# Pairing the small-expert steps of a mixture-of-experts layer, and folding their partial sums behind the pair

## The chip, the core and the metric

The kernel runs on one core of a Trainium2 chip. The core has a matrix engine (PE, TensorE), three elementwise engines (DVE, ACT and POOL) and sixteen DMA engines, whose transfers are issued here by the SP queue and, for a few, by ACT. The engines run side by side and wait for each other through semaphores. The metric is the device time of one execution in microseconds (us).

## The reference

Two transformer layers over 256 latent tokens and 256 context tokens of width 1024. Each layer has a token mixer (neighbourhood attention, differential attention, short convolution) and a feed-forward part; layer 0 has a dense one, layer 1 a mixture of eight experts of which each token takes two. The change lies in that last part and in the final normalization:

```python
def swiglu(h, w1, w3, w2):
    return (jax.nn.silu(h @ w1) * (h @ w3)) @ w2          # 1024 -> 3584 -> 1024 in an expert

def moe_ffn(h, w_router, w1, w3, w2):
    logits = jnp.einsum('...d,de->...e', h, w_router)
    top_vals, top_idx = lax.top_k(logits, 2)
    top_w = jax.nn.softmax(top_vals, axis=-1)
    gates = jnp.sum(jax.nn.one_hot(top_idx, 8) * top_w[..., None], axis=-2)
    y = jnp.zeros_like(h)
    for e in range(8):
        y = y + gates[..., e:e + 1] * swiglu(h, w1[e], w3[e], w2[e])
    return y
...
x_lat = x_lat + g_f * moe_ffn(modulate(rms_norm(x_lat), sh_f, sc_f), ...)
return rms_norm(x_lat, final_gain)
```

All weights are fp32, so the experts' weights are by far the largest stream: 44 MB for one expert.

## The kernel before

The first half of the program (to about 870 us) is layer 0 and the mixer of layer 1; the change doesn't touch it. Then `route` sorts the experts by how many tokens chose them and gives each a rank. For the inputs used here the branch in `moe_main` (line 1846) is taken that treats ranks 0 and 1 as *heavy*, ranks 7, 2, 3, 4 and 5 as *light*, and leaves rank 6, which no token chose, out. Rank 7 is always expert 0, so that its weights can be fetched before the routing is known.

**Heavy experts** (`heavy`) are computed for all 256 tokens. Each 128x1024 piece of weights is cut into a rounded part `whi` (ACT, line 469) and the rest `wlo` (DVE, line 471), and each product is done as three fast ones (lines 222 to 224, tile `H`): `xh*whi`, `xl*whi`, `xh*wlo`. The pieces are cut one ahead of their use, in three buffers. One piece gives 24 products of 256 columns (first two weight matrices) or 12 of 512 columns (third matrix, where the operands are `gh`, `gl`). Groups of four 512-column blocks of PSUM are filled at a time (`by_bank`); the last two pieces of a group are used together, bank by bank, and so both must be cut before the second product set of that step.

**Light experts** (`light`) gather at most 32 or 64 tokens (`n` = 64 for rank 2, 32 for the others) and use the weights uncut, in plain fp32. With so few tokens the array is cut into column tiles: four tiles of 32 columns or two of 64, which work side by side on different rows of the weights, so that one PSUM bank (tile `L`) holds four (or two) partial sums. A plain fp32 product is two instructions in the profile. When a bank is done, ACT copies it to `s` (line 1649, `folded`), and later a *fold* sums the partial sums: products of `s` with a matrix of ones at the right places (tile `tg`), for `n` = 32 in four column tiles with a DVE transpose behind them (lines 1657 and 1661, tile `sT`, two buffers), for `n` = 64 as four full-width products with `s` as the loaded operand (line 1665). The result goes to `g`: by ACT with Silu for the first matrix (line 1668), by a DVE multiplication for the second (line 1670).

One light expert is 21 *steps* (the generator's `yield`s). A step (`quad`) uses four chunks of 512 KB. Steps 0 to 11 are pairs: steps 2k and 2k+1 fill the same two banks. Steps 12 and 13 fill one bank each. Steps 14 to 20 are the third matrix and fill two banks together. After step 20 the result is scattered to the tokens (`scatter`): it is scaled (`of`), cut into `oh` and `ol` (lines 469 and 471), and each token half gets two fast products with `selT` (lines 1528 and 1529), added to `xk` (tile `xT`) on DVE. The folds that wait are emitted after the first step of the next bank pair (`fold_all` at `u == 0`). `places` (transposes and small products that make `selT`, lines 1454 and 1456) and the gather of the next rank's tokens (line 1469) are small tasks put between steps by `some_tasks`.

**The order.** `mix_experts` weaves the two streams: a surplus of PE time over transfers decides whether a heavy step or light steps come next; light steps come in bursts of two (`BURST`), whatever bank they belong to. First eight steps of rank 7 run before the weave (`first_steps`). The products of both streams are chained in this written order; a scheduler then places every engine's instructions. Twenty 512 KB buffers (tile `raw`) form one ring for both streams: SP issues the next transfer when the oldest buffer is free.

**The end** (`finish_out`): squares of the result are summed on ACT, DVE multiplies all four quarters by the final gain, then 1/rms is worked out in small DVE steps, and two quarters are scaled by it on DVE and two on ACT, and stored.

Of the kernel before, what the change touches and what calls it, by code (L numbers as in the profile page):

```python
# [13 lines left out]
F32 = mybir.dt.float32  # L14
F32R = mybir.dt.float32r
# [8 lines left out]
KT = 8  # L24
# [15 lines left out]
PE_COST = {32: (1.05, 1.0), 64: (1.95, 1.9), 128: (3.75, 3.65)}  # L40
HEAVY = 2.85
WIN_W = 16
BURST = 2
GROUPS = (2, 2, 2, 1)


# [83 lines left out]
def tile_hybrid_block(ctx: ExitStack, tc: tile.TileContext, x, c, cx, c_ctx, ada_w, ada_b, w_in, w_out, na_rpb,  # L130
# [1239 lines left out]

    def first_steps():

        run = mo["run7"] = light((7,), 32)
        while len(mo["early"]) > TAIL:
            next(run)
            mo["run7_done"] = mo.get("run7_done", 0) + 1
        while mo["folds"]:
            mo["folds"].popleft()()
        mo["run7_tasks"] = list(tasks)
        tasks.clear()  # L1380
        mo["far"].close()
        mo["left"], mo["early"] = mo["early"], {}

    def pbank(tag):
        return mo["psum"].tile([128, 512], F32, name=tag, tag=tag, bufs={"H": 4, "L": 2, "tg": 2}[tag])
# [130 lines left out]
    def scatter(o, h, selT, gate, after):  # L1516

        big = mo["big"]
        of = gated(o, h, gate)
        oh = big.tile([128, 512], F32R, name="oh", tag="oh", bufs=2)  # L1520
        ol = big.tile([128, 512], F32R, name="ol", tag="ol", bufs=2)
        parts(of.rearrange("p a b -> p (a b)"), oh, ol)

        def add():
            for t in range(2):
                y = pbank("tg")
                s = selT[:, t * 128:(t + 1) * 128]
                pe.matmul(y, s, oh, start=True, stop=False)  # L1528
                pe.matmul(y, s, ol, start=False, stop=True)  # L1529
                accumulate(t, h, y.rearrange("p (a b) -> p a b", a=4))  # L1530
            if after is not None:
                after(h)
        mo["adds"].append(add)
        tasks.append(lambda: mo["adds"] and mo["adds"].popleft()())
# [88 lines left out]
    def light(ranks, n, last=None):  # L1623
# [16 lines left out]
        for i, r in enumerate(ranks):  # L1640
            v = {}

            def place(r=r, v=v):
                v["v"] = places(r, n)
            chunks = light_chunks(r)

            def folded(a, j, first):
                s = mo["pool"].tile([128, 512], F32, name="s", tag="s", bufs=2)
                act.activation(s, a, AF.Copy)  # L1649

                def fold():

                    gs = g[j]
                    p = pbank("tg")[:, :4 * n].rearrange("p (a b) -> p a b", a=4)
                    if n == 32:
                        for c in range(4):
                            chained(pe.matmul(p[32 * c:32 * c + 32], fold32,  # L1657
                                              s.rearrange("p (q c i) -> p c q i", c=4, i=32)[:, c], start=True,
                                              stop=True, tile_position=(0, 32 * c), skip_group_check=True))
                        t = mo["pool"].tile([128, 4, n], F32, name="sT", tag="sT", bufs=2)  # L1660
                        dve.transpose(out=t, in_=p)  # L1661
                        p = t
                    else:
                        for f in range(4):
                            chained(pe.matmul(p[:, f, :], s[:, f * 128:(f + 1) * 128], mo["fold", n], start=True,
                                              stop=True))
                    if first:
                        act.activation(gs, p, AF.Silu)
                    else:
                        dve.tensor_tensor(out=gs, in0=gs, in1=p, op=ALU.mult)  # L1670
                folds.append(fold)

            def fold_all():
                while folds:
                    folds.popleft()()

            def quad(banks, lhs, u, nk, per):

                raws = [weights(*next(chunks)) for _ in range(4)]
                for h, bank_ in enumerate(banks):  # L1680
                    for k in range(4 * per):
                        cs = (h if per == 1 else k % 2) * 512
                        product(bank_, lhs(4 * per * u + k), raws[k // per][:, cs:cs + 512], 4 * per * u + k, nk)

            def latents(kt, i=i):
                return x[:, kt, i * n:(i + 1) * n]

            def columns(f):
                return g[f // 4][:, f % 4, :]
            for j0, nj in col_groups(GROUPS):  # L1690
                for w in range(2):
                    a = [pbank("L") for _ in range(nj)]
                    for u in range(nj):
                        quad(a, latents, u, KT, 3 - nj)
                        if u == 0 and not (nj == 1 and w):
                            fold_all()
                        if u < nj - 1:
                            yield
                    for h in range(nj):
                        folded(a[h], j0 + h, w == 0)  # L1700
                    yield
                if j0 == 2:
                    tasks.append(place)
            end = i == len(ranks) - 1
            if end:
                mo["following"]()
            o = [pbank("L") for _ in range(2)]
            for u in range(7):
                quad(o, columns, u, 28, 1)
                if u == 0:  # L1710
                    fold_all()
                if u < 6:
                    yield
            if "v" not in v:
                tasks.remove(place)
                place()
            while mo["adds"]:
                mo["adds"].popleft()()
            for h in range(2):
                scatter(o[h], h, *v["v"], last if end else None)  # L1720
            yield

    def mix_experts(heavies, lights, end=True, begun=False):
# [3 lines left out]

        def pool(name, **kw):
            return s.enter_context(tc.tile_pool(name=name, side="right", **kw))
        mo["tight"] = any(n == 128 for _, n in lights)  # L1730
        if heavies:
            mo["split"] = pool("m_split", bufs=2 if mo["tight"] else 3)
# [39 lines left out]
        runs = {"light": light_groups()}  # L1772
        if heavies:
            runs["heavy"] = heavy(last, heavies)
        parts_of = {"heavy": deque([(HEAVY, 0.5)] * (84 * len(heavies))),
                    "light": deque((2 * PE_COST[n][k >= 14], 2.0) for r, n in lights for _ in r for k in range(21))}
        if begun:
            tasks.extend(mo["run7_tasks"])
            for _ in range(mo["run7_done"]):
# [4 lines left out]
        mean = sum(p[0] for p in both) / sum(p[1] for p in both)  # L1784

        total, surplus = len(both), START
        k, burst = "heavy", 0
        while runs:
            done = total - sum(len(q) for q in parts_of.values())
            lead = LEAD * max(done, 0) / total  # L1790

            if "heavy" not in runs or "light" not in runs:
                k = next(iter(runs))
            elif burst == 0:
                k = "heavy" if surplus <= lead else "light"
                burst = BURST if k == "light" else 1
            burst -= 1
            if next(runs[k], "end") == "end":
                del runs[k]
                continue  # L1800
            cost, load = parts_of[k].popleft()
            surplus += cost - mean * load
            if "heavy" not in runs:
                tasks.extend(gains)
                gains = []
            some_tasks(1 if len(tasks) < 4 else 2)
# [13 lines left out]

    def finish_out():
        squares(1)
        qs = {}
        for t in range(2):
            for h in range(2):
                hs = slice(4 * h, 4 * h + 4)
                q = qs[t, h] = mo["ring"][t][:, h, :].rearrange("p (k n) -> p k n", k=4)
                dve.tensor_tensor(out=q, in0=mo["xk"][t][:, hs, :], in1=mo["fg"][:, hs, :], op=ALU.mult)
        ms = sm(2)
        dve.tensor_tensor(out=ms, in0=mo["ss"][:, 0:2], in1=mo["ss"][:, 2:4], op=ALU.add)  # L1830
        dve.tensor_scalar(out=ms, in0=ms, scalar1=1.0 / D, scalar2=None, op0=ALU.mult)
        r = rsqrt(ms, 2)
        for t in range(2):
            for h in range(2):
                q = qs[t, h]
                if h:
                    act.activation(q, q, AF.Copy, scale=r[:, t:t + 1])
                else:
                    dve.tensor_scalar(out=q, in0=q, scalar1=r[:, t:t + 1], scalar2=None, op0=ALU.mult)
                (act if h else sy).dma_start(  # L1840
                    out=out[0, t * 128:(t + 1) * 128, h * 512:(h + 1) * 512].rearrange("p (k n) -> p k n", k=4), in_=q)

    def moe_main():
        route()
# [79 lines left out]
```

## Time and profile before

| | |
|---|---|
| time, median of 3 runs | 1692.32 us (1688.62 to 1694.82) |
| the profiled execution | 1694.52 us, of which the profile's span is 1692.7 us |
| PE busy | 1630.3 us, 96% of the span |
| DVE, ACT busy | 1026.3 us (61%), 639.4 us (38%) |
| bytes read from HBM | 431.66 MB, 256 GB/s over the span |
| granted PE clock, mean | 0.986 of full speed |

Times in rows count from the span's start. In a timeline row the second number is the length of the row's instructions together; products overlap, so that what a run of products costs PE is read from its start to the start of the next row. In `x16` the last number counts instructions.

### The profile page before, as it was taken

To read this page: it belongs to the slowest core of one execution; us is meant where nothing else is said; L and a number is where in the kernel's file an instruction comes from. 1 tells how busy PE (TensorE), PEld (TensorE's weight loads), DVE (VectorE), ACT (ScalarE), POOL (GpSimd) and SP (SyncE) were. 2 spreads that over 40 slices of the span, in tenths; PEclk is the share of its full clock that TensorE was granted. 3 is DMA by queue.
4 is the path that set the end of the run, shared out by engine and by line. 5 is a ranking of instruction groups with operands and counts; after the bars stand their busy time and mean duration, and the time that the engine had idled before them with its cause. 6 is when DMAs were issued, how large, how long until landed. Compare 5 with 4: busy or idle time off the path is not lost. (4 is left out here: it accounts for less than half of the span.)

```text
span 1692.7 us, 28524 instructions
## 1 busy us (share of the span) xinstructions
PE 1630.3 (96%) x10942; PEld 1268.0 (75%) x10942; DVE 1026.3 (61%) x2043; ACT 639.4 (38%) x1057; POOL 25.6 (2%) x43
## 2 busy tenths in 40 slices
PE   7999999999999999999989999999999999999996
PEld 4688777988778888988874866666878677878773
DVE  4768977888877784779963343214445545353454
ACT  4555544422212222465534322313333243333431
POOL 0100001000000000000010000000000000000000
PEclk9999999999999999999989999999999999999998
DMA  9743444266545553342499999989999989998994
GB/s 286 178 126 109 104 149 112 84 191 199 199 154 168 170 192 112 100 125 75 178 365 366 409 407 355 344 336 403 363 362 396 368 335 377 394 398 335 389 381 176
DMA packets 234193, 434.66 MB, mean 257 GB/s; under 512 B 23497, under 2 KB 142785, under 8 KB 234049
## 3 DMA queue, kind: packets, MB, share of 16 engines
q1 hardware_dynamic: 232560, 432.14, 71.5%
q8 instruction: 88, 1.44, 0.4%
q10 hardware_dynamic: 1488, 0.62, 0.1%
q14 instruction: 57, 0.46, 0.1%
HBM read 431.66 MB, written 1.05 MB: 256 GB/s over the span
## 5 line engine op out<-in xcount | busy, mean ns | idle before, releaser
L471 DVE TENSOR_TENSOR wlo<-raw,whi 128x1024 fp32r<-128x1024 f32 x168 | 202.9, 1223 | 235.7 <-ACT whi L469 218.9
L222 PE MATMUL H<-xh,whi 128*128 128x256 f32 x896 | 257.7, 288 | 2.6 <-ACT whi L469 1.8
L224 PE MATMUL H<-xh,wlo 128*128 128x256 f32 x896 | 254.9, 284 | 2.0 <-DVE wlo L471 1.9
L223 PE MATMUL H<-xl,whi 128*128 128x256 f32 x896 | 254.6, 284 | 0.0
L469 ACT ACTIVATE whi<-raw 128x1024 fp32r<-128x1024 f32 x168 | 174.3, 1054 | 181.9 <-PE H L223 92.4
L222 PE MATMUL mm<-hh,whi 128*128 128x512 f32 (+1 forms) x648 | 230.2, 356 | 1.7 <-ACT t2k L298 1.2
L223 PE MATMUL mm<-hl,whi 128*128 128x512 f32 (+1 forms) x648 | 226.4, 350 | 0.0
L224 PE MATMUL mm<-hh,wlo 128*128 128x512 f32 (+1 forms) x648 | 225.1, 348 | 0.0
L100 ACT ACTIVATE whi<-raw 128x1024 fp32r<-128x1024 f32 x130 | 134.6, 1056 | 238.6 <-DMA raw<-in_ffn_w_dram 139.4
L101 DVE TENSOR_TENSOR wlo<-raw,whi 128x1024 fp32r<-128x1024 f32 x130 | 157.1, 1220 | 56.5 <-ACT whi L100 55.6
L222 PEld LDWEIGHTS H<-xh,whi 128*128 128x128 f32 x896 | 172.5, 192 | 20.0 <-issue 9.3
L224 PEld LDWEIGHTS H<-xh,wlo 128*128 128x128 f32 x896 | 172.6, 193 | 3.0 <-DVE wlo L471 3.0
L223 PEld LDWEIGHTS H<-xl,whi 128*128 128x128 f32 x896 | 172.7, 193 | 0.2
L222 PEld LDWEIGHTS mm<-hh,whi 128*128 128x128 f32 x648 | 123.5, 191 | 21.3 <-ACT t2k L298 2.8
L1636 PE MATMUL L<-raw,xT 128*32 128x512 f32 (+1 forms) x896 | 137.2, 597 | 0.3
L224 PEld LDWEIGHTS mm<-hh,wlo 128*128 128x128 f32 x648 | 123.3, 191 | 15.1 <-issue 0.2
L223 PEld LDWEIGHTS mm<-hl,whi 128*128 128x128 f32 x648 | 123.8, 191 | 13.6
L322 DVE SCALAR_TENSOR_TENSOR ada_t<-raw,scol,ada_t 128x256 f32<-128x256 f32 x266 | 116.5, 480 | 2.8
L1649 ACT ACTIVATE s<-L 128x512 f32<-128x512 f32 x70 | 41.8, 597 | 151.0 <-PE L L1636 127.1
L222 PE MATMUL H<-whi,gh 128*128 128x512 f32 x224 | 90.2, 403 | 3.9 <-ACT gh L469 3.1
L1661 DVE STREAM_TRANSPOSE sT<-tg 128x128 f32<-128x128 f32 x56 | 15.5, 308 | 126.4 <-PE tg L1657 126.3
L223 PE MATMUL H<-wlo,gh 128*128 128x512 f32 x224 | 88.7, 396 | 0.9 <-DVE wlo L471 0.9
(320 smaller groups left out, 2764.2 us busy)
## 6 DMA issues: line engine op xcount, KB each, us to landing
raw<-in_moe_w_dram SPq DMA_DIRECT2D x572, 512.0 KB, 8.3
raw<-in_ada_w_dram SPq DMA_DIRECT2D x40, 1024.0 KB, 5.3
raw<-in_ffn_w_dram SPq DMA_DIRECT2D x32, 1024.0 KB, 5.4
raw<-in_w_in_dram SPq DMA_DIRECT2D x12, 1024.0 KB, 5.2
raw<-in_w_in_dram SPq DMA_DIRECT2D x24, 512.0 KB, 5.3
aw<-in_ada_w_dram SPq DMA_DIRECT2D x16, 512.0 KB, 7.3
far<-in_moe_w_dram SPq DMA_DIRECT2D x16, 512.0 KB, 7.3
raw<-in_w_out_dram SPq DMA_DIRECT2D x5, 1024.0 KB, 5.6
```

The lines of the kernel that those rows point to most:

```text
L100: self.nc.scalar.activation(hi, r, AF.Copy)
L101: self.nc.vector.tensor_tensor(out=lo, in0=r, in1=hi.bitcast(F32), op=ALU.subtract)
L222: return [pe.matmul(o, ah, bh, start=start, stop=False, **kw), pe.matmul(o, ah, bl, start=False, stop=False, **kw), pe.matmul(o, al, bh, s ...
L223: pe.matmul(o, ah, bl, start=False, stop=False, **kw),
L224: pe.matmul(o, al, bh, start=False, stop=stop, **kw)]
L322: dve.scalar_tensor_tensor(out=t[:, g, :], in0=raw[:, kt, :], scalar=scol[:, kt, g:g + 1], in1=t[:, g, :], op0=ALU.mult, op1=ALU.add)
L469: act.activation(hi, src, AF.Copy, scale=scale)
L471: dve.tensor_tensor(out=lo, in0=src, in1=hi.bitcast(F32), op=ALU.subtract)
L1636: chained(pe.matmul(o[c * n:(c + 1) * n, :], lhs, rhs, start=(k < ng), stop=(k >= nk - ng), tile_position=(0, c * n), skip_group_check=True))
L1649: act.activation(s, a, AF.Copy)
L1661: dve.transpose(out=t, in_=p)
```

## The change

Six edits, all behind the routing:

1. A light burst no longer counts two steps: it goes on until a step that ends a bank pair (odd steps, and step 20, which is a burst by itself).
2. Steps 12 and 13 fill two banks that are held together; their folds come after both.
3. Waiting folds are emitted after the *second* step of a pair (`u == 1`) and no longer after the first; only where light steps run without heavy ones (`mo["alone"]`: `first_steps`, and branches not taken here) it stays at the first.
4. The fold for `n` = 64 also goes in column tiles of 32, in two halves of the columns, with two DVE transposes; `sT` has one buffer instead of two.
5. The scatter of the very last light rank isn't cut in `oh` and `ol`: one plain fp32 product with `of` takes the place of two.
6. In `finish_out` only two quarters are multiplied by the gain early; the other two are scaled and multiplied in one DVE instruction at the end.

```diff
-BURST = 2
...
     def first_steps():
+        mo["alone"] = True
...
     def scatter(o, h, selT, gate, after):
-        parts(of.rearrange("p a b -> p (a b)"), oh, ol)
+        of = of.rearrange("p a b -> p (a b)")
+        if after is None:
...
+            parts(of, oh, ol)
...
+                if after is None:
+                    pe.matmul(y, s, oh, start=True, stop=False)
+                    pe.matmul(y, s, ol, start=False, stop=True)
+                else:
+                    pe.matmul(y, s.bitcast(F32), of, start=True, stop=True)
...
-                    if n == 32:
...
-                        t = mo["pool"].tile([128, 4, n], F32, name="sT", tag="sT", bufs=2)
-                        dve.transpose(out=t, in_=p)
+                    if n < 128:
+                        t = mo["pool"].tile([128, 4, n], F32, name="sT", tag="sT", padded_shape=[128, 4, 64])
+                        p = p.rearrange("p (a b) -> p a b", b=32)
+                        for h in range(n // 32):
+                            for c in range(4):
+                                chained(pe.matmul(p[32 * c:32 * c + 32, 4 * h:4 * h + 4, :],
+                                                  mo["fold", n][:, 32 * h:32 * h + 32],
+                                                  s.rearrange("p (q c i) -> p c q i", c=4, i=32)[:, c], start=True,
+                                                  stop=True, tile_position=(0, 32 * c), skip_group_check=True))
+                            dve.transpose(out=t[:, :, 32 * h:32 * h + 32], in_=p[:, 4 * h:4 * h + 4, :])
...
             for j0, nj in col_groups(GROUPS):
+                if nj == 1:
+                    a = [pbank("L") for _ in range(2)]
+                    for w in range(2):
+                        quad(a[w:w + 1], latents, 0, KT, 2)
+                        if w == 0:
+                            yield
+                    fold_all()
+                    for w in range(2):
+                        folded(a[w], j0, w == 0)
+                    yield
+                    continue
                 for w in range(2):
...
-                        if u == 0 and not (nj == 1 and w):
+                        if u == (0 if mo["alone"] else 1):
                             fold_all()
...
             for u in range(7):
                 quad(o, columns, u, 28, 1)
-                if u == 0:
+                if u == (0 if mo["alone"] else 1):
                     fold_all()
...
+                    "light": deque((2 * PE_COST[n][k >= 14], 2.0, k % 2 == 1 or k == 20) for r, n in lights for _ in r
+                                   for k in range(21))}
...
-            elif burst == 0:
+            elif whole:
                 k = "heavy" if surplus <= lead else "light"
-                burst = BURST if k == "light" else 1
-            burst -= 1
...
-            cost, load = parts_of[k].popleft()
+            cost, load, whole = parts_of[k].popleft()
...
     def finish_out():
...
+        for t in range(2):
+            dve.tensor_tensor(out=qs[t][0], in0=mo["xk"][t][:, 0:4, :], in1=mo["fg"][:, 0:4, :], op=ALU.mult)
...
         for t in range(2):
+            act.activation(qs[t][0], qs[t][0], AF.Copy, scale=r[:, t:t + 1])
+            dve.scalar_tensor_tensor(out=qs[t][1], in0=mo["xk"][t][:, 4:8, :], scalar=r[:, t:t + 1],
+                                     in1=mo["fg"][:, 4:8, :], op0=ALU.mult, op1=ALU.mult)
```

What this moves is seen in the order of the instructions. The first place is PE where rank 3 ends: its last step (the `g` products), the scatter of its result (`oh`, `ol` with `selT`), and the first step of rank 4 (the `xT` products of 32 rows). Before:

```order
L1636 MATMUL L<-raw_8687,g 32x512
L1636 MATMUL L<-raw_8691,xT 32x512
L1528 MATMUL tg<-oh,selT 128x512 x2
L1636 MATMUL L<-raw_8695,xT 32x512
L1529 MATMUL tg<-ol,selT 128x512 x2
L1636 MATMUL L<-raw_8699,xT 32x512
L1528 MATMUL tg<-oh,selT 128x512
L1529 MATMUL tg<-ol,selT 128x512
L1528 MATMUL tg<-oh,selT 128x512
L1529 MATMUL tg<-ol,selT 128x512
L1636 MATMUL L<-raw_8703,xT 32x512
```

and now:

```order
L1641 MATMUL L<-raw_8687,g 32x512
L221 MATMUL H<-xh,whi 128x256
L222 MATMUL H<-xl,whi 128x256
L223 MATMUL H<-xh,wlo 128x256
L221 MATMUL H<-xh,whi 128x256
L222 MATMUL H<-xl,whi 128x256
L223 MATMUL H<-xh,wlo 128x256
L1531 MATMUL tg<-oh,selT 128x512 x2
L221 MATMUL H<-xh,whi 128x256
L222 MATMUL H<-xl,whi 128x256
```

Step 20 now ends its burst, and the scatter's full-width products stand between full-width heavy products instead of between the light ones in column tiles.

The second place is ACT at the first fold of rank 3 (`s` the copies out of the banks, `g` the Silu of the fold, `whi` the cut of the next heavy pieces). Before:

```order
L469 ACTIVATE whi<-raw_8699 128x1024
L469 ACTIVATE whi<-raw_8703 128x1024
L1668 ACTIVATE g<-sT 128x128 x2
L1649 ACTIVATE s<-L 128x512 x2
L469 ACTIVATE whi<-raw_8739 128x1024
L469 ACTIVATE whi<-raw_8743 128x1024
```

and now:

```order
L468 ACTIVATE whi<-raw_8703 128x1024
L1654 ACTIVATE s<-L 128x512
L1677 ACTIVATE g<-sT 128x128
L1654 ACTIVATE s<-L 128x512
L1677 ACTIVATE g<-sT 128x128
L468 ACTIVATE whi<-raw_8739 128x1024
```

The two Silu stood ahead of the copies of the pair being filled; now they stand between and behind them, since the fold comes after the pair, and the cut of the next heavy piece stays behind all four.

The third place is PE at the first fold of rank 2. Before:

```order
L1636 MATMUL L<-raw_8683,xT 64x512
L1636 MATMUL L<-raw_8687,xT 64x512
L1665 MATMUL tg<-fold_8762,s 128x64 x8
L222 MATMUL H<-whi,gh 128x512
L223 MATMUL H<-wlo,gh 128x512
```

and now:

```order
L1641 MATMUL L<-raw_8707,xT 64x512
L1641 MATMUL L<-raw_8711,xT 64x512
L1665 MATMUL tg<-s,fold_8762 32x128 x16
L221 MATMUL H<-whi,gh 128x512
L222 MATMUL H<-wlo,gh 128x512
```

Eight full-width products of 64 columns become sixteen of 128 columns in tiles of 32.

## Rows read from the trace of the kernel before

**Rows 1.** Busy time by stretch: PE, weight loads, DVE, ACT, POOL; clock, DMA share, GB/s.
```profile
930.00:1000.00 70.00, 69.91 (x532) 54.60 (x531) 29.52 (x38) 23.74 (x30) 0.00 (x0) 1.00 1.03 409
1400.00:1500.00 100.00, 100.00 (x771) 77.00 (x770) 45.42 (x59) 37.49 (x47) 0.00 (x0) 1.00 1.00 387
```

**Rows 2.** Timeline of PE at rank 3's first fold: start, length, line, out<-in, idle before.
```profile
1176.00 1.92 PE L1636 MATMUL L<-raw,xT 128*32 128x512 f32 x16
1177.74 0.62 PE L1657 MATMUL tg<-s,fold 128*32 128x128 f32 x16
1178.18 1.90 PE L1636 MATMUL L<-raw,xT 128*32 128x512 f32 x16
1180.01 0.51 PE L222 MATMUL H<-whi,gh 128*128 128x512 f32 x1
...
1181.81 0.50 PE L222 MATMUL H<-whi,gh 128*128 128x512 f32 x1 [0.83 <-ACT whi L469]
1183.07 0.51 PE L223 MATMUL H<-wlo,gh 128*128 128x512 f32 x1 [0.76 <-DVE wlo L471]
```

**Rows 3.** Timeline of all engines in the same stretch, ACT's and DVE's rows.
```profile
1178.56 0.53 ACT L1668 ACTIVATE g<-sT 128x128 f32<-128x128 f32 x2 [6.83 <-DVE sT L1661]
...
1180.22 0.60 ACT L1649 ACTIVATE s<-L 128x512 f32<-128x512 f32 x1 [0.26 <-PE L L1636]
...
1180.71 1.99 ACT L469 ACTIVATE whi<-raw 128x1024 fp32r<-128x1024 f32 x2
1181.79 2.36 DVE L471 TENSOR_TENSOR wlo<-raw,whi 128x1024 fp32r<-128x1024 f32 x2 [3.05 <-ACT whi L469]
```

**Rows 4.** Timeline of PE at rank 2's first fold.
```profile
1020.62 2.00 PE L1665 MATMUL tg<-fold,s 128*128 128x64 f32 x16
1022.43 0.48 PE L222 MATMUL H<-whi,gh 128*128 128x512 f32 x1
```

**Rows 5.** Timeline of PE: first and last rows of four light bursts, and a scatter.
```profile
937.64 1.92 PE L1636 MATMUL L<-raw,g 128*32 128x512 f32 x16
...
947.45 0.38 PE L222 MATMUL H<-xh,whi 128*128 128x256 f32 x1
...
995.02 1.92 PE L1636 MATMUL L<-raw,g 128*32 128x512 f32 x16
...
1005.21 0.50 PE L222 MATMUL H<-whi,gh 128*128 128x512 f32 x1
...
1232.68 1.92 PE L1636 MATMUL L<-raw,xT 128*32 128x512 f32 x16
...
1238.37 0.39 PE L222 MATMUL H<-xh,whi 128*128 128x256 f32 x1
...
1250.08 1.92 PE L1636 MATMUL L<-raw,xT 128*32 128x512 f32 x16
...
1334.62 1.92 PE L1636 MATMUL L<-raw,g 128*32 128x512 f32 x16
...
1341.23 0.40 PE L1529 MATMUL tg<-ol,selT 128*128 128x512 f32 x1
1341.46 0.40 PE L1528 MATMUL tg<-oh,selT 128*128 128x512 f32 x1
...
1343.86 0.39 PE L222 MATMUL H<-xh,whi 128*128 128x256 f32 x1
```

**Rows 6.** Timeline of all engines behind the last light product, at the end.
```profile
1674.67 1.53 DVE L1508 SCALAR_TENSOR_TENSOR of<-L,gate,gf 128x512 f32<-128x512 f32 x2 [6.43 <-PE L L1636]
...
1680.31 0.69 DVE L1514 TENSOR_TENSOR xT<-xT,tg 128x512 f32<-128x512 f32 x1 [0.17 <-PE tg L1529]
...
1680.91 2.49 DVE L1828 TENSOR_TENSOR raw<-xT 128x512 f32<-128x512 f32 x4
...
1681.62 0.19 ACT L1818 ACTIVATION_READ_ACCUMULATOR s<-xT 128x1 f32 x1
...
1686.13 1.33 ACT L1837 ACTIVATE raw<-raw,sm 128x512 f32<-128x512 f32 x2 [4.32 <-issue]
```

More of the change, by code (lines that the diff above doesn't have):

```diff
@@ L1519, in scatter @@
         of = gated(o, h, gate)
-        oh = big.tile([128, 512], F32R, name="oh", tag="oh", bufs=2)
-        ol = big.tile([128, 512], F32R, name="ol", tag="ol", bufs=2)
-        parts(of.rearrange("p a b -> p (a b)"), oh, ol)
+        of = of.rearrange("p a b -> p (a b)")
+        if after is None:
+            oh = big.tile([128, 512], F32R, name="oh", tag="oh", bufs=2)
+            ol = big.tile([128, 512], F32R, name="ol", tag="ol", bufs=2)
+            parts(of, oh, ol)
         def add():
@@ L1527, in add @@
                 s = selT[:, t * 128:(t + 1) * 128]
-                pe.matmul(y, s, oh, start=True, stop=False)
-                pe.matmul(y, s, ol, start=False, stop=True)
+                if after is None:
[3 more added lines that the diff above has]
+                    pe.matmul(y, s.bitcast(F32), of, start=True, stop=True)
                 accumulate(t, h, y.rearrange("p (a b) -> p a b", a=4))
@@ L1653, in fold @@
                     gs = g[j]
-                    p = pbank("tg")[:, :4 * n].rearrange("p (a b) -> p a b", a=4)
-                    if n == 32:
[L1656 to L1659, printed above, removed]
-                        t = mo["pool"].tile([128, 4, n], F32, name="sT", tag="sT", bufs=2)
-                        dve.transpose(out=t, in_=p)
+                    p = pbank("tg")[:, :4 * n]
+                    if n < 128:
[8 more added lines that the diff above has]
+                            dve.transpose(out=t[:, :, 32 * h:32 * h + 32], in_=p[:, 4 * h:4 * h + 4, :])
                         p = t
                     else:
+                        p = p.rearrange("p (a b) -> p a b", a=4)
                         for f in range(4):
@@ L1690, in light @@
             for j0, nj in col_groups(GROUPS):
+                if nj == 1:
[9 more added lines that the diff above has]
+                    continue
                 for w in range(2):
-                    a = [pbank("L") for _ in range(nj)]
-                    for u in range(nj):
-                        quad(a, latents, u, KT, 3 - nj)
-                        if u == 0 and not (nj == 1 and w):
+                    a = [pbank("L") for _ in range(2)]
+                    for u in range(2):
+                        quad(a, latents, u, KT, 1)
+                        if u == (0 if mo["alone"] else 1):
                             fold_all()
-                        if u < nj - 1:
+                        if u == 0:
                             yield
-                    for h in range(nj):
+                    for h in range(2):
                         folded(a[h], j0 + h, w == 0)
@@ L1729, in pool @@
             return s.enter_context(tc.tile_pool(name=name, side="right", **kw))
+        mo["alone"] = not heavies
         mo["tight"] = any(n == 128 for _, n in lights)
@@ L1774, in mix_experts @@
             runs["heavy"] = heavy(last, heavies)
-        parts_of = {"heavy": deque([(HEAVY, 0.5)] * (84 * len(heavies))),
-                    "light": deque((2 * PE_COST[n][k >= 14], 2.0) for r, n in lights for _ in r for k in range(21))}
+        parts_of = {"heavy": deque([(HEAVY, 0.5, True)] * (84 * len(heavies))),
+                    "light": deque((2 * PE_COST[n][k >= 14], 2.0, k % 2 == 1 or k == 20) for r, n in lights for _ in r
+                                   for k in range(21))}
         if begun:
@@ L1786, in mix_experts @@
         total, surplus = len(both), START
-        k, burst = "heavy", 0
+        k, whole = "heavy", True
         while runs:
@@ L1822, in finish_out @@
         squares(1)
-        qs = {}
+        ms = sm(2)
+        qs = [[mo["ring"][t][:, h, :].rearrange("p (k n) -> p k n", k=4) for h in range(2)] for t in range(2)]
         for t in range(2):
[L1825 to L1829, printed above, removed]
+            dve.tensor_tensor(out=qs[t][0], in0=mo["xk"][t][:, 0:4, :], in1=mo["fg"][:, 0:4, :], op=ALU.mult)
         dve.tensor_tensor(out=ms, in0=mo["ss"][:, 0:2], in1=mo["ss"][:, 2:4], op=ALU.add)
@@ L1833, in finish_out @@
         for t in range(2):
+            act.activation(qs[t][0], qs[t][0], AF.Copy, scale=r[:, t:t + 1])
+            dve.scalar_tensor_tensor(out=qs[t][1], in0=mo["xk"][t][:, 4:8, :], scalar=r[:, t:t + 1],
+                                     in1=mo["fg"][:, 4:8, :], op0=ALU.mult, op1=ALU.mult)
             for h in range(2):
[L1835 to L1841, printed above, removed]
+                (sy if h else act).dma_start(
+                    out=out[0, t * 128:(t + 1) * 128, h * 512:(h + 1) * 512].rearrange("p (k n) -> p k n", k=4),
+                    in_=qs[t][h])
     def moe_main():
```

## The prediction, made before the changed kernel was timed

> **What bounds the kernel now.** I read the busy times by stretch first, then PE's timeline burst by burst, then ACT and DVE around the few places where PE stands still. In the part that the change touches PE is busy without a break: 100.00 of 100 us in one stretch, 69.91 of 70 in another [rows 1]. DMA is close behind it, at a share of 1.00 with 387 GB/s; that this is not yet its limit is seen in the other stretch, where it moved 409 GB/s. DVE is busy for 45 and ACT for 37 of 100 us. So what counts is how long PE needs for each light burst, and whether the burst leaves ACT and DVE too late with the next heavy piece. Both can be read at one burst [rows 2]: 1.74 us for sixteen light products, 0.44 for sixteen fold products, 1.83 for the next sixteen, 4.01 in all; and behind it four heavy products that take from 1180.01 to behind 1183.07, because the second heavy piece wasn't cut.
>
> The sum is made against the profiled execution (1694.52 us), which is 2.2 us above the median of the runs; I subtract it from the median, 1692.3.
>
> **Bursts that were already pairs: nothing.** Ranks 7, 3 and 5 started their bursts on even steps. With the fold moved behind, the same 32 light and 16 fold products follow each other in one block: 1.74 + 1.74 + 0.44 and once the 0.09 by which a change of tiles is dearer (1.83 against 1.74 [rows 2]). That is the same 4.01. For ranks 2 and 4 the fold stood behind the second step already.
>
> **Rank 2's folds: -5.8 us.** Sixteen full-width products took 1.81 us, from 1020.62 to 1022.43 [rows 4]; there are seven such pairs of folds. Now it is 32 in tiles of 32, at the rate of the 0.44 for sixteen [rows 2]: 0.88, and 0.1 for the change of tiles. 7 x (1.81 - 0.98) = 5.8. The 28 new transposes on DVE are of the form that rank 3's folds have; they lie in DVE's idle half.
>
> **Bursts that were torn: -9.6 us.** Where full-width products stood between light ones, each change drained the tiles and left them half empty [rows 5].
> - Rank 3's scatter: 1334.62 to 1343.86, 9.24 us for 16 + 16 light products and eight scatter products. Now they are 16 light alone (1.83), eight scatter products between heavy ones at 0.23 (the two rows from 1341.23), and rank 4's last step, which becomes a burst by itself (1.83): 5.5. Saves 3.7.
> - Rank 7's scatter: 995.02 to 1005.21, 10.19 us. Now 1.83 + 1.84 + 3.5 for rank 2's last step (two tiles instead of four: twice the 1.74): 7.2. Saves 3.0.
> - The gather for rank 2: 937.64 to 947.45, 9.81 us. Now a burst of 4.01, and 32 gather products at the price of products of the same form, 1.81/16 = 0.113 [rows 4]: 7.6. Saves 2.2.
> - The `places` of ranks 3 and 5: 1232.68 to 1238.37, 5.69 us each. Now 4.01 and six small products, 0.7. Saves 1.8 together.
>
> That is 10.7. Scatter products among heavy ones wait in PE's queue if `oh` or `ol` comes late, and then a heavy product waits behind them; I give back 1.1. Bounds: 10.7 if nothing waits; nothing at all if each of the five places waits 2 us, which is what the stall in rows 2 cost.
>
> **The new waits at Silu folds: +4.2 us.** A heavy piece takes PE 2.93 us (1238.37 to 1250.08 for four). Let T be the time at which a pair's fold starts. Silu ran 0.82 behind it (1177.74 and 1178.56) [rows 2, 3]. Now ACT has in order: first Silu (to T+1.1), the second bank's copy (0.5 more, as 1180.22 to 1180.71), second Silu (0.3), and only then `whi` and, behind it, DVE's `wlo`, 1.0 and 1.2 each [rows 3]: ready at T+4.1. Heavy products start at T+0.55 and want `wlo` of the next but one piece 2.93 + 0.24 later, at T+3.7. PE, behind which everything is queued, stands for 0.4 to 0.5 us. Before, the cut started 0.7 behind the first heavy product (1180.71 against 1180.01); now it is about 1.35. The single `sT` buffer doesn't add to it, since the second Silu waits for the copy longer than for the transpose. Thirteen pairs of folds have a Silu and copies behind it; three come where both next pieces are cut already, one is counted below: 9 x 0.47 = 4.2. Bounds: 0, if the cut is further ahead than I think, and 13 x 2.1.
>
> **Pairs that now fall before a double piece: +3.7 us.** In rows 2 four heavy products, 0.93 us at 0.23, took 3.06: 2.1 lost, as the last two pieces of a group are wanted together. In the new order that burst stays there (0.5 worse, by the Silu), and two of rank 4's pairs now come to stand before such a step. Their folds have no Silu, so the cut starts at about 0.15 instead of 0.7 behind the first heavy product: 2.1 - 0.55 = 1.6 each. 0.5 + 3.2 = 3.7. Bounds: 0 and 2 x 2.1 + 0.5.
>
> **The end: -1.9 us.** Before, 6.2 us lay between the last light product and DVE's free time at 1680.91 [rows 6]. Now PE needs only `of`, not `oh` and `ol`; but an fp32 product is two instructions of 0.43 (four rounds in 1.74, rows 2), 0.86 for each of four, and they wait for two PSUM buffers. I get the last addition at 0.65 us earlier. Behind it stood four multiplications, 2.49, to 1683.40, while ACT's squares were done at 1681.81 [rows 6]: now the two that are left stand between the additions, and the squares end the wait: 1.5 saved. At the end two instructions of DVE like the 1.53 in rows 6 take the place of ACT's 1.33 as the last: 0.2 back. Bounds: 0.9 and 2.9.
>
> Sum: -5.8 - 9.6 + 4.2 + 3.7 - 1.9 = -9.4. 1692.3 - 9.4 = **1682.9 us**.
>
> **Rivals.**
> - *No new waits.* If ACT and DVE are further ahead than I read them, the two positive terms go: -17.3, 1675.0. For it: before, PE stood still at one pair of folds only by more than a few tenths. Against it: 1180.71 is late already, and the change makes it later.
> - *The transfers become the limit.* At 387 GB/s and a share of 1.00 [rows 1] the ring hasn't much to give, and PE's gain would come back as waits for `raw`. What remains is the end and what the peak of 409 allows, about half of the rest: -1.9 - 3.7, near 1687. Against it: the stretch with 409 GB/s had PE at 69.91 of 70 too.
> - *The tearing moves, it doesn't go.* Scatter products in the heavy stream wait for ACT and DVE as long as the light ones drained. Then the 9.6 goes: +0.2, 1692.5.
> - *The copies out of PSUM bind.* Each of the thirteen Silu pairs loses what the burst in rows 2 lost, 2.1 us: 27.3 instead of 4.2, 1706. It decides from 1.05 us for each pair on, (9.4 + 4.2)/13: there the gain is gone, and above it the kernel is slower. For it: the mechanism is the same as in rows 2, ACT's copy ahead of the cut. Against it: there the double piece was next; elsewhere a whole piece of 2.93 us lies between.
>
> The last one has a rule beside it. The Trainium skill, page "TensorEngine Tiling (Array Packing)", section "PSUM Bottleneck", says that tiling speeds up TensorE but not the evacuation of PSUM, and that after a fourfold speedup the copy may become the bottleneck. By that rule rank 2's faster folds would end in waits for `sT` and `g`, and the time would be that of this rival. The trace so far agrees at one burst, by 2.1 us, and disagrees at the others.
>
> **How the numbers follow.** My forecast, with terms a few us either way, 0.55; no new waits 0.20; transfers 0.12; tearing moved 0.06; copies bind 0.07. A measurement of this kernel tells about 0.5% from no change, that is 8.5 us. Of the forecast's 0.55 a little over half lies beyond that (its middle is -9.4): with the 0.20, faster 0.50. Same: the other part, the transfers and the tearing, 0.43. Slower 0.07. The range for 8 in 10 is 1674 to 1692.5: from a little below the sum without any wait to the one without the torn bursts.
>
> **What would show it.** In the new profile: each of rank 2's seven folds one row of 32 products in tiles of 32 and 0.98 us to the next heavy row; bursts of 32 light products unbroken; scatter products between `H` rows, without idle time before them; behind Silu folds a wait of PE for `wlo` of 0.3 to 0.6 us; two waits of 1.6 in rank 4; DVE's `sm` row directly behind ACT's accumulator at the end. I am wrong if PE waits for `raw`, or if waits for `wlo` behind folds sum to over 15 us or to nothing.

## The result, and the profile after

The changed kernel takes 1704.29 us (median of 7 runs, 1698.9 to 1710.16), against 1692.32 for the kernel before: a ratio of 1.0068, 95% interval 1.005 to 1.0087. It is slower, by 0.7%, where 9.4 us less were forecast. Its profiled execution took 1704.29 us, with a span of 1702.5.

The largest loss is in one stretch, that of rank 2's folds. This is the view by windows, first of the kernel before and then of the kernel after (columns as in [rows 1]; the second window of after is one short piece of the first):

```profile
1020.00:1120.00 100.00, 100.00 (x653) 68.63 (x650) 23.98 (x32) 25.39 (x38) 0.00 (x0) 1.00 0.95 360
```

```profile
1020.00:1120.00 100.00, 89.61 (x660) 56.02 (x658) 27.50 (x49) 25.32 (x36) 0.00 (x0) 0.95 0.86 324
1043.40:1046.80 3.40, 3.40 (x22) 3.06 (x21) 0.74 (x2) 0.60 (x1) 0.00 (x0) 0.50 1.03 413
```

PE, busy for 100.00 of 100 us before, now stands for 10.4, and its granted clock falls from 1.00 to 0.95. In the short window it is 0.50, 1.2 GHz, and PE is fully busy there: this is slow work, no idle time. Three such pieces of 3.4 us lie in this part of the trace (from 1043.4, 1094.6 and 1111.7), each behind the longer wait inside a fold; at half speed each costs about 1.7. Transfers fell to 324 GB/s with a share of 0.86, and no row of PE in this stretch waits for `raw`, so that they bind nothing.

The timeline of all engines at rank 2's first fold in the kernel after, the place of [rows 4] (start, length, what ran, idle time before it and what ended it):

```profile
1024.15 0.43 PE L1665 MATMUL tg<-s,fold 128*32 128x128 f32 x8
1024.72 0.32 DVE L1669 STREAM_TRANSPOSE sT<-tg 128x128 f32<-128x128 f32 x1 [5.31 <-PE tg L1665]
1025.10 0.64 PE L1665 MATMUL tg<-s,fold 128*32 128x128 f32 x16 [0.52 <-DVE sT L1669]
1025.59 0.32 DVE L1669 STREAM_TRANSPOSE sT<-tg 128x128 f32<-128x128 f32 x1 [0.55 <-PE tg L1665]
...
1026.14 0.41 ACT L1677 ACTIVATE g<-sT 128x256 f32<-128x256 f32 x1
1026.58 0.32 DVE L1669 STREAM_TRANSPOSE sT<-tg 128x128 f32<-128x128 f32 x1 [0.68 <-ACT g L1677]
1026.95 0.43 PE L1665 MATMUL tg<-s,fold 128*32 128x128 f32 x8 [1.21 <-DVE sT L1669]
1027.31 0.50 PE L221 MATMUL H<-whi,gh 128*128 128x512 f32 x1
```

The products come as 8, 16 and 8, not as 32. The second half of a fold waits 0.52 for the transpose of the first half, and the last eight wait 1.21: their turn comes behind the second fold's first transpose, which waits for Silu to read the one `sT` buffer. The pair takes 3.16 us (1024.15 to 1027.31), where it took 1.81 [rows 4] and 0.98 was forecast. The waits of PE at fold and heavy products from 920 to 1660 in the kernel after (total, times, longest) show where it stands in all:

```profile
PE tg L1665 <- DVE sT L1669: 9.5, 12, 1.6
PE H L221 <- ACT whi L468: 3.6, 3, 1.5
PE H L221 <- ACT gh L468: 3.1, 2, 1.6
PE H L223 <- DVE wlo L470: 2.3, 5, 0.8
PE H L222 <- DVE wlo L470: 2.2, 4, 0.8
PE H L223 <- DVE gl L470: 1.2, 2, 0.6
```

And the same view of the kernel before:

```profile
PE H L222 <- ACT gh L469: 3.1, 2, 1.6
PE H L224 <- DVE gl L471: 1.2, 2, 0.6
PE H L224 <- DVE wlo L471: 1.1, 1, 1.1
PE H L223 <- DVE wlo L471: 0.9, 2, 0.8
PE H L222 <- ACT whi L469: 0.8, 1, 0.8
PE H L222 <- DVE of L1508: 0.8, 1, 0.8
```

The first row of the kernel after is new and is the largest. The two rows for `gh` and `gl` belong to waits that the kernel before has too.

The rest of the change did what it was read to do. A gather and a scatter that had torn light bursts [rows 5], in PE's timeline of the kernel after:

```profile
939.68 3.64 PE L1641 MATMUL L<-raw,g 128*32 128x512 f32 x32
943.14 0.62 PE L1665 MATMUL tg<-s,fold 128*32 128x128 f32 x16
944.03 3.74 PE L1469 MATMUL tg<-selG,hk 128*128 128x64 f32 x32
...
1344.42 1.92 PE L1641 MATMUL L<-raw,g 128*32 128x512 f32 x16
...
1347.10 0.73 PE L1531 MATMUL tg<-oh,selT 128*128 128x512 f32 x2
1348.26 0.64 PE L1532 MATMUL tg<-ol,selT 128*128 128x512 f32 x2
```

Light and fold products go through in one piece, the gather stands by itself, and the scatter products go two by two between heavy ones. Some `places` products (those of rank 3) still stand inside a light burst. The new waits at a Silu fold (first row) and, in rank 4, before a double piece (the step that uses the last two pieces of a group together):

```profile
1380.47 0.39 PE L223 MATMUL H<-xh,wlo 128*128 128x256 f32 x1 [0.38 <-DVE wlo L470]
1397.97 0.39 PE L221 MATMUL H<-xh,whi 128*128 128x256 f32 x1 [1.05 <-ACT whi L468]
1399.23 0.39 PE L223 MATMUL H<-xh,wlo 128*128 128x256 f32 x1 [0.76 <-DVE wlo L470]
```

And the end, on DVE and ACT, the place of [rows 6]:

```profile
1686.17 1.58 DVE L1508 SCALAR_TENSOR_TENSOR of<-L,gate,gf 128x512 f32<-128x512 f32 x2 [8.40 <-PE L L1641]
...
1692.74 0.19 ACT L1838 ACTIVATION_READ_ACCUMULATOR s<-xT 128x1 f32 x1
1692.96 0.16 DVE L1847 TENSOR_TENSOR sm<-sm 128x2 f32<-128x2 f32 x1 [0.85 <-ACT s L1838]
...
1695.73 1.33 ACT L1851 ACTIVATE raw<-raw,sm 128x512 f32<-128x512 f32 x2 [2.80 <-DVE sm L236]
```

From `of` to the start of the last scaling it is 9.56 us, and was 11.46 (1674.67 to 1686.13 [rows 6]); the squares now end the wait. The last scaling is now DVE's, 1.41 us where ACT's took 1.33, so that 1.8 is saved.

### The profile page after: what moved, and what is told of

It reads as the page before. It is cut to its first block, busy times and chain, and to the rows that moved or that the text cites. A ratio compares the mean times of both kernels' runs of the same rounds, so it can differ in the third digit from the quotient of the medians.

```text
span 1702.5 us, 28773 instructions
## 1 busy us (share of the span) xinstructions
PE 1624.5 (95%) x11054; PEld 1263.3 (74%) x11054; DVE 1036.7 (61%) x2067; ACT 634.7 (37%) x1055; POOL 24.7 (1%) x43
## 3 DMA queue, kind: packets, MB, share of 16 engines
HBM read 431.66 MB, written 1.05 MB: 254 GB/s over the span
## 5 line engine op out<-in xcount | busy, mean ns | idle before, releaser
L1669 DVE STREAM_TRANSPOSE sT<-tg 128x128 f32<-128x128 f32 x84 | 26.5, 316 | 217.4 <-PE tg L1665 208.0
L221 PEld LDWEIGHTS mm<-hh,whi 128*128 128x128 f32 x648 | 123.0, 190 | 21.4 <-ACT t2k L297 2.8
L223 PEld LDWEIGHTS mm<-hh,wlo 128*128 128x128 f32 x648 | 123.1, 190 | 15.1 <-issue 0.2
L1641 PE MATMUL L<-raw,xT 128*32 128x512 f32 (+1 forms) x896 | 126.3, 595 | 0.0
```

Source lines behind the costliest of these rows:

```text
L221: return [pe.matmul(o, ah, bh, start=start, stop=False, **kw), pe.matmul(o, ah, bl, start=False, stop=False, **kw), pe.matmul(o, al, bh, s ...
L223: pe.matmul(o, al, bh, start=False, stop=stop, **kw)]
L1641: chained(pe.matmul(o[c * n:(c + 1) * n, :], lhs, rhs, start=(k < ng), stop=(k >= nk - ng), tile_position=(0, c * n), skip_group_check=True))
L1669: dve.transpose(out=t[:, :, 32 * h:32 * h + 32], in_=p[:, 4 * h:4 * h + 4, :])
```

## The experiments

Every kernel ran in five rounds beside the kernel before, 5 to 12 times in all. Ratios are to the kernel before, with 95% intervals.

**a1_full_fold**: rank 2's fold as before, the rest changed.

```diff
-                    if n < 128:
+                    if n == 32:
```

> The changed kernel with rank 2's fold back in its old full-width form (no transposes for it), all else as changed. Theory A (the tiled fold itself is what went wrong: 3.16 us for a pair of folds at 1024.15 to 1027.31 in the changed kernel, 1.81 before): 7 x 1.35 = 9.5 us come back, and with them the stretches of 3.4 us at half the granted clock at 1043, 1095 and 1112, about 1.7 each: 1689 to 1695. Rival B (the pairs and their new order cost what was gained, through copies, Silu and cuts that come late): the fold's form matters by 1 or 2 us, 1702 to 1704.

Measured 1693.01 us, ratio 1.0007 (0.9994 to 1.002). As theory A has it: 11.3 us of the loss are the fold, and B falls. What is left of the change gains nothing, though, where 3.6 were forecast for it.

**a2_products_first**: the same 32 products and four transposes, in another order.

```diff
                             for c in range(4):
                                 chained(pe.matmul(p[32 * c:32 * c + 32, 4 * h:4 * h + 4, :],
...
+                        for h in range(n // 32):
                             dve.transpose(out=t[:, :, 32 * h:32 * h + 32], in_=p[:, 4 * h:4 * h + 4, :])
```

> The changed kernel with the products of both column halves written ahead of both transposes, so that the order has 32 fold products in a row; sT keeps its one buffer. Theory A (products of the second half stand behind the transpose of the first, on PE's queue): the pair of folds takes 0.9 to 1.1 us and not 3.16, 7 x 2.1 = 14.7 less, and the falls of the clock behind them go, up to 5: 1684 to 1690. Rival C (one buffer of sT is what PE waits for, or the transposes themselves bind): still 1698 or more. Rival B: 1702 to 1704.

Measured 1687.87 us, ratio 0.9977 (0.9967 to 0.9988): 16.4 below the changed kernel, by order alone. PE's timeline at rank 2's first fold:

```profile
1025.53 1.08 PE L1665 MATMUL tg<-s,fold 128*32 128x128 f32 x32
1026.55 0.50 PE L221 MATMUL H<-whi,gh 128*128 128x512 f32 x1
```

One row of 32, 1.02 us to the next heavy product. Rival C falls: `sT` still has one buffer, and its second transpose still waits for Silu, but nothing of PE's is queued behind it.

**a3_two_sT**: a second place for `sT`, the order as in the changed kernel.

```diff
+                        if n == 64 and j % 2:
+                            t = mo["x7"].rearrange("p k n -> p (k n)").rearrange("p (a b) -> p a b", a=4)
```

> The changed kernel, in which every other fold of rank 2 is transposed into a second place (rank 7's gathered tokens, not needed any more), as if sT had two buffers. Theory A: the first wait of each fold (0.5 to 0.65 us, for the transpose of the half before) stays, the second (1.2 to 1.75 us, in which the transpose waits for Silu to read sT) shrinks to about 0.5, the same as the first, in the four folds with Silu: 4 x 0.9 = 3.6 and one or two falls of the clock: 1697 to 1702. Rival C (the one buffer is the cause of all of it): both waits go, 1688 to 1692. Rival B: 1702 to 1704.

Measured 1694.81 us, ratio 1.0016 (1.0007 to 1.0025), 2 to 7 us better than theory A said. The waits and the window in its trace:

```profile
PE tg L1667 <- DVE x L1671: 3.6, 5, 0.9
PE tg L1667 <- DVE sT L1671: 3.2, 7, 0.5
```

```profile
1020.00:1120.00 100.00, 92.29 (x712) 54.07 (x708) 27.31 (x51) 25.30 (x36) 0.00 (x0) 1.00 0.91 341
```

All twelve waits are still there, as theory A has it, with 6.8 us together for 9.5. What it missed is the clock: with waits of at most 0.9 it stayed at 1.00 in this stretch, and none of the three half-speed pieces came. All runs together say the same. As an estimate, half speed costs a run its span times what its mean granted clock lacks to 1; that is 25 us on average in the changed kernel and 19.6 in a3, so that over 5 of the 9.5 us are clock.

**b1_fold_only** and **b2_fold_only_first**: the kernel before with the tiled fold alone, in the changed kernel's order and with products first (the edits are those of the change's fold and of a2).

> The kernel before with nothing changed but rank 2's fold, in the new form (two halves, each with its transpose behind it, one buffer of sT). Theory A: 7 x 1.35 = 9.5 us slower, and up to 5 more if the clock falls behind the waits as in the changed kernel: 1700 to 1707. Rival B: the fold alone costs 1 or 2 us, 1692 to 1694.

> The kernel before with nothing changed but rank 2's fold, tiled, with its products ahead of both transposes. Theory A (the forecast's term of -5.8 us was right for 32 products in one row; the order within the fold is what failed): 1686 to 1688, against 1707.6 with each half's transpose between. Rival F (half of the loss of that kernel is the transposes and the one buffer, whatever the order): 1693 to 1700.

b1 measured 1707.58 us, ratio 1.0097 (1.0079 to 1.0116), just above what theory A allowed; b2 1687.42, ratio 0.9964 (0.995 to 0.9978). The same edit costs 15 us or gives 5.5, by where the transposes stand. In b1 the waits are the changed kernel's:

```profile
PE tg L1660 <- DVE sT L1664: 10.9, 12, 2.0
```

**b3_end_only**: the kernel before with the last scatter unsplit and the final scaling as changed.

> The kernel before with only the end changed: the last scatter unsplit, two quarters scaled and multiplied in one instruction. The forecast: 1.9 us less (bounds 0.9 and 2.9), 1689.4 to 1691.4. By the trace of the changed kernel nearer to 1: from the last run of light products to the first small step on DVE 15.8 us without the gain products, against 16.7 before. Rival: no change, because the plain fp32 products at the end cost what the squares give: 1692.

Measured 1691.09 us, ratio 0.9991 (0.9977 to 1.0006). The middle is the forecast's, 1.8 less; the interval doesn't exclude no change, and the 1.8 in the trace (above) is the better witness.

**c1_start_fold**: a2, and the moved folds only from the first heavy step on.

```diff
-        mo["alone"] = not heavies
+        mo["alone"] = True
...
+            if k == "heavy":
+                mo["alone"] = False
             if next(runs[k], "end") == "end":
```

> The changed kernel with products first (as a2_products_first, 1687.9 us), and until the first heavy step the waiting folds stay behind the first step of a pair; one pair of rank 7 is moved by it, no other. Theory D (the part of the forecast that still fails is the start of the heavy stream: the moved fold puts two Silu and two copies straight before the first cut, the first heavy product starts 31.15 us behind rank 7's first light product and not 29.03, and the granted clock then lies at half for 6.8 us, which before didn't happen): 2.1 us and 2.5 to 3.4 of the clock come back, 1682.5 to 1684. Rival E (it isn't the start; the pairs cost about 5 us more than forecast all along the weave): 1687 to 1688.

Measured 1682.30 us, ratio 0.9934 (0.9909 to 0.9959), just below theory D's range. The place in the changed kernel first, then in this one:

```profile
909.76 5.56 PE L1641 MATMUL L<-raw,x 128*32 128x512 f32 x48
...
915.14 0.62 PE L1665 MATMUL tg<-s,fold 128*32 128x128 f32 x16
...
917.06 1.99 ACT L468 ACTIVATE whi<-raw 128x1024 fp32r<-128x1024 f32 x2
...
918.15 0.39 PE L221 MATMUL H<-xh,whi 128*128 128x256 f32 x1 [2.39 <-ACT whi L468]
```

```profile
909.96 3.85 PE L1641 MATMUL L<-raw,x 128*32 128x512 f32 x32
913.63 0.62 PE L1665 MATMUL tg<-s,fold 128*32 128x128 f32 x16
...
916.66 1.99 ACT L468 ACTIVATE whi<-raw 128x1024 fp32r<-128x1024 f32 x2
...
917.76 0.39 PE L221 MATMUL H<-xh,whi 128*128 128x256 f32 x1 [1.80 <-ACT whi L468]
```

The wait is 0.59 shorter, not the 2.1 that I had read. The rest is the clock: the windows of a2 and of c1 show 0.50 and 1.00 for the same 6.8 us.

```profile
918.80:925.60 6.80, 6.04 (x31) 5.09 (x34) 1.91 (x2) 0.47 (x1) 0.00 (x0) 0.50 1.05 404
```

```profile
918.80:925.60 6.80, 6.58 (x66) 4.05 (x70) 1.30 (x2) 0.00 (x0) 0.00 (x0) 1.00 1.04 401
```

Half the speed for 6.8 us costs 3.4, and with 0.6 gives 4.0 of the 5.6 between a2 and c1. By the estimate from the mean clock of all runs (21.5 us in a2, 15.1 in c1) the clock is all of it. That the fold's place makes the clock fall is not shown: the profiled execution of a1 has the fold in the same late place and no fall at the start, while those of c2 and d1 have it early, as in c1, and 3.4 us at half there. A second pair of runs gives less for the place: a1 and d1 differ in it and in the end, by 1.6 us, and with 1.8 for the end 3.4 are left.

**c2_folds_first**: a2, and no fold moved behind the pair anywhere (only the first line of c1's edit).

> As a2_products_first, with the folds behind the first step of each pair everywhere, so that no copies and Silu of a pair stand close together before a cut. Theory D: the start gives 4 to 5 us, the waits behind Silu folds about 2 (five waits of 0.38 to 0.46), the waits before double pieces 0.6; the gathers stand among light products again and cost 2 to 4: 1682 to 1685. Rival E': the waits at double pieces and behind Silu folds don't hang on the fold's place, and only the torn bursts come back: 1690 or more.

Measured 1686.21 us, ratio 0.9955 (0.9939 to 0.9971), 1 us above theory D's range. The waits behind Silu folds are gone, but the products of gathers and `places` tear light bursts again. c1, which moves them away from the start, is 3.9 better in the median, with intervals that overlap.

**d1_pairs_only**: c1 without the new fold and the new end.

> The pairs alone: the kernel c1_start_fold (1682.3 us) with rank 2's fold back in the full-width form of before and the end as before. By the sums so far 1682.3 + 5.5 + 1.8 = 1689.6, 3.3 less than before. Theory G (torn bursts give what was forecast, about 10 to 11 us of PE time in light products, and 6 to 8 of it go in waits behind the pairs and in more changes between the streams): 1688 to 1691. Rival H (the parts don't add: the pairs gain nothing or lose without the new fold): 1692 to 1695.

Measured 1691.39 us, ratio 0.9992 (0.9978 to 1.0006): 1.5 less in the middle, just above theory G's range; by the interval (3.7 less to 1.0 more) it may be nothing.

**d2_two_ahead** and **d3_before_two_ahead**: c1, and the kernel before, with heavy pieces cut two ahead.

```diff
-        ready.append(next(todo))
-        while ready:
-            v = next(todo, None)
-            if v is not None:
-                ready.append(v)
-            yield ready.popleft()
+        while True:
+            while len(ready) <= mo["depth"]:
...
+            yield ready.popleft()
...
+            mo["depth"] = 1
             two = [next(pieces) for _ in range(2)]
+            mo["depth"] = 2
```

> c1_start_fold with heavy pieces cut two ahead of their use and not one (three buffers hold them; at a double piece it goes back to one ahead). Theory I (the waits before double pieces, 2.21, 1.81 and 1.86 us, and the five of 0.38 to 0.46 behind Silu folds come from cuts that start only when the burst has ended): nearly all of the 7.9 us go, 1674 to 1677. Rival J (ACT and DVE do the cuts in order with the copies, and a cut further ahead comes before the copies and Silu that rank's products need, or the transfers bind): 1681 to 1684.

> The kernel before with heavy pieces cut two ahead, nothing else changed. Theory I: the two waits that the cut ends, 1.59 us at 1181.81 and 1.92 at 1521.90, with the clock's fall behind each (3.4 us at half, 1.7 lost) go: 1692.9 - 3.5 - 3.4 = 1686 to 1688. Rival J: 1692 to 1694.

d2 measured 1669.09 us, ratio 0.9864 (0.9842 to 0.9886): faster than both kernels. PE's waits at heavy products in its weave, behind the first heavy step:

```profile
PE H L221 <- ACT gh L468: 3.1, 2, 1.6
PE H L223 <- DVE gl L470: 1.2, 2, 0.6
PE H L222 <- DVE wlo L470: 0.5, 1, 0.5
PE H L223 <- DVE wlo L470: 0.4, 1, 0.4
```

No wait for `whi` is left (3.6 us in the changed kernel). Theory I said 1674 to 1677. The gain of 13.2 on c1 is larger than its 7.9. Counted from the start of one product to the start of the next, PE loses 15.1 us at heavy products in c1's weave and 6.2 in d2's, 8.9 less; the mean clock gives about 1 more, and some 3 stay open. d3 measured 1689.32, ratio 0.9982 (0.997 to 0.9994), a gain of 3.6 where theory I said 5 to 7. The stop of [rows 2] is gone in it, but the other one that theory I named is not (0.81 and 1.11 at 1520.44 and 1522.78, with the clock at half behind it), and PE waits 0.76 for `oh` at two scatters that tear light bursts. Whether the pairs are needed for the gain of d2 was not tried apart.

## Why the prediction was wrong, point by point

The forecast was 1682.9 and the changed kernel took 1704.3. Of the 21.4 us between, 16.4 is the order within rank 2's folds (changed kernel less a2) and 5.6 what c1 gains at the start of the heavy stream (a2 less c1); c1, free of both, stands at 1682.3. That this is so near the forecast is in part luck, as the terms for the pairs show.

- **"Rank 2's folds: -5.8 us"** is the step that failed. It took 32 products "at the rate of the 0.44 for sixteen", as one row. The written order has each half's transpose inside the loop over halves, and the second half's products write the tile that it reads. The transposes were costed at nothing because they "lie in DVE's idle half"; DVE was idle, but PE stood queued behind each of them: 9.5 us of waits for `sT`, none forecast. Of the signs that the forecast named, this one failed, a row of 8, 16 and 8 for one of 32; none of its signs of being wrong came (in the weave PE never waits for `raw`, and its waits for `wlo` sum to 4.5 us). The size was right for the row assumed: 1.02 for 0.98, and b2 measures 5.5 less for 5.8. The sentence that the single `sT` buffer adds nothing holds at the Silu waits it spoke of; within rank 2's folds, which it didn't consider, the buffer costs 9.5 of the 16.4 (a3). Whether a PSUM bank of its own for each half would have spared PE the waits was not tried.
- **The clock.** The forecast had no term for it. A wait was priced by its length, but behind three of the fold waits PE also ran at half speed for 3.4 us. The trace of the kernel before had it already, right behind the stop of [rows 2], and the forecast passed over it:

```profile
1183.50:1186.90 3.40, 3.40 (x10) 2.61 (x9) 1.68 (x3) 0.00 (x0) 0.00 (x0) 0.50 1.03 412
```

From 900 to 1665 the kernel before has two such pieces and the kernel after six. By the mean clock of all runs half speed costs 25 us in the changed kernel and 20.5 in the one before, 4.5 of the 12.0 that it lost.

- **"The new waits at Silu folds: +4.2 us"** was too high in the weave, 0.38 to 0.46 at five places instead of 0.47 at nine, and put nothing on the pair before the first heavy step, where no piece is cut beforehand. There two copies and two Silu stand ahead of the first cut, and the wait for it is 2.39 instead of 1.80.
- **"Pairs that now fall before a double piece: +3.7 us"**: at the two new places PE waits 1.81 (1.05 + 0.76, shown above) and 1.86; from start to start, as the forecast counted, 2.1 and 2.3 are lost, against 1.6. It had no term for the stop of 0.80 + 1.12 at 1521.90 in the kernel before, which has no counterpart after.
- **"Bursts that were torn: -9.6 us"**: the places that were read in the trace cost what was forecast. The gather's burst takes 4.01 and the gather 3.54, together 7.6; rank 3's scatter products take 0.25 each for 0.23; rank 3's burst with `places` takes 4.86 for 4.7. (Two such bursts save 2.0 by the forecast's own numbers, not its 1.8.) With the two terms above, net, the pairs were forecast at -1.7, and d1 measures -1.5, which is in part luck: from start to start PE lost 9.6 us at such waits before and 15.1 in d1, 5.5 more and not 7.9, so that the sum would be -4.1, outside d1's interval. What takes the rest is open.
- **"The end: -1.9 us"**: 1.8 in the trace and in b3.
- **The rivals.** The copies out of PSUM, whose 1706 lies near the time, were not the cause: they would have lost 2.1 us at each Silu pair, and the weave shows about 0.4. The Trainium skill, page "TensorEngine Tiling (Array Packing)", section "PSUM Bottleneck", says that PSUM's evacuation may become the limit behind faster tiles. The trace agrees as to the place (12 waits for `sT`, 9.5 us); a2, with the same products and the same evacuation, has no such wait, so what bound was their order. The transfers were not the limit, at 324 GB/s in the stretch that lost. New waits did come, and no scatter product between heavy ones waits, so the two other rivals fall too.

## What to carry to other kernels

Before pricing a block of products by its rate, go through the written order and look for another engine's instruction that reads their tile between them: work off the critical path costs nothing only if nothing of the bound engine is queued behind it. Write all products of a group first, then what reads them. Look apart at the first step of a stream, where nothing is prepared, and where such waits remain try to prepare one step further ahead: it gave 13.2 us on c1 here, 3.6 on the kernel before.

## What the runs showed of the hardware that was not expected

Waits of PE of 0.8 to 2.4 us were at times followed by 3.4 or 6.8 us at half the granted clock, which cost about as much as the wait itself. Not each such wait was: in the changed kernel the stop for `gh` and `gl` of 1.55 + 0.61 us comes twice, and only behind the second, near 1657, did the clock fall. Changing the order within a fold moved 16.4 us, though the waits for `sT` sum to 9.5. By the mean clock of all runs 3.5 of it is the clock (25 us less 21.5), and a wait costs more than its idle time: the pair of folds shown takes 2.14 us more than a2's, with 1.73 of waits in it.
